# A hybrid encoder layer on one core: first keys' transpose later, own value buffers for every other of the last units, layer results stored by ScalarE, last row block in two column halves

## The chip, the cores and the metric

The kernel runs on one core of a Trainium2 chip. The engines of the core are TensorE (PE, with PEld for its weight loads), VectorE (DVE), ScalarE (ACT), GpSimd (POOL) and SyncE (SP), which in this kernel issues nearly all of the transfers; 16 DMA engines carry these out. Each engine works through its own list of instructions in order and waits on semaphores for the others. The metric is the device time of one launch in microseconds (us); less is better.

## The reference

Two sequences of 2048 tokens (prompt and sample, width 1024) go through one layer with the same weights:

```python
h = rms_norm(x, norm_w)
q_a, k_a, v_a, g_a, q_b, k_b, v_b, g_b = split(h @ w_in)      # 512 128 128 512 512 512 512 512
q_a, k_a = (partial_rope(rms_norm(u)) for u in (q_a, k_a))
o_a = windowed_gqa_sink(q_a, k_a, v_a, sink_a) * silu(g_a)    # 8 q heads, 2 kv heads, +-128 tokens
o_b = neighbourhood_attn(rms_norm(q_b), rms_norm(k_b), v_b, rpb_b) * silu(g_b)   # 8 heads, 64-wide grid, 8 rows x 16 columns
x = x + concat([o_a, o_b]) @ w_out
y = x + (p @ w_ple) * sigmoid(x @ w_ple_gate)                 # p: 256 wide
```

Everything is float32.

## The kernel before

All matrix products run as pairs of rounded numbers: each operand is split into a high and a low part (`[:, a]`, `[:, b]` with 0 and 1), and three of the four partial products are summed in PSUM. So "hi/lo" splits on ACT and DVE belong to every operand, and a product over 128 of the inner dimension takes three matmuls, shown as `x3`.

The program has three stages. **Stage A** (units f = 0 to 31, until about 708 us) takes one tile of 128 tokens per unit through group A: projections in `proj_a`, attention in `unit_a`. **Stage B** (units 32 to 95, until about 1821 us) does the same for group B, half of its 8 heads at a time, in `proj_b` and `unit_b`. **Stage C** (until the end) is the output projection and then the gate, in 8 groups of 7 products (Strassen's way of multiplying 2 x 2 blocks) with four row blocks `mi` each. A row block of 128 x 512 takes 12 matmuls on PE.

PE runs in the order in which the program is written. While PE works on the attention of a unit, it is handed matmuls of other work between the attention's steps: the projections of later units, as a stream that two tables of fractions of a unit (PLAN_A, PLAN_B) cut into pieces. From unit 90 on no projections are left, and the stream is `ple_ahead`: `p @ w_ple`, 8 row blocks for each of 8 tiles of 512 tokens. A row block is 6 matmuls into the PSUM tile `pple`, a copy by ACT into a buffer `ev` (L1003) and a store of 256 KB into the DRAM tensor `ple_d`, from which stage C reads it back at the end. Buffers `ev` come from two rings of 3 and 2; after stage B (`tail`) from another ring.

In the order of the other engines, `P(...)` marks instructions that keep their place in program order, and the rest is arranged by the tile scheduler by priorities and readiness.

The places that the change touches:

- `proj_a` and `keys_a`: the keys of unit f are normalised and rotated on POOL and DVE into `kt` (L517 to L520), and when `ka` matmuls of the same projection have passed, PE transposes them into `pkt` (L255) and ACT and DVE write them to `ks_a`. `ka` is 33 (KA), and 22 in the units in `last`.
- `unit_b`, `load_values` (L861 to L868): up to four loads of values, each 240 to 256 KB, from `v_d` into tiles `vw`, which lie in two rings, `vp` with 3 and `vr_` with 2 buffers. SP issues them. A unit's work on PE ends in `pob` matmuls, one group for each pair of heads, which need `vw` and the transposed probabilities `p_t`: PE transposes into `ptb`, ACT casts the high part (L894), DVE subtracts for the low part (L895).
- `prep_b` (L836 to L839): the queries of the next unit, from the PSUM tile `pqtb`: two times ACT (`q1b`), DVE (`q`) and POOL.
- `store_ple` (L976 to L982): the store of a copy `ev` goes out when the next one has been made, on SP.
- `product`, `result` and `behind_tanh` (L1213 to L1288): in stage C's gate groups the last sum of a row block is followed by ACT's tanh (L1273), and two DVE operations (L1283, L1284), which make the sigmoid, the product with `p @ w_ple` and the sum with x, out of it; then SP stores 256 KB of y (L1288). DVE's part of a row block is written behind the next row block's tanh, the last one's by a call at the end (L1325).

Of the kernel before, what the change touches and what calls it, by code (L numbers as in the profile page):

```python
# [11 lines left out]
F32 = mybir.dt.float32  # L12
F32R = mybir.dt.float32r
# [6 lines left out]
NT = SEQ // 128  # L20
# [80 lines left out]
def emit(ctx, tc, io):  # L101
# [382 lines left out]
    def proj_a(f):  # L484
        s, t = divmod(f, NT)
        xr, ms, (ssq, ee) = xt.pop(f), ms_a[:, f:f + 1], stats.pop(f)
        ka = 22 if f in last else KA
        early = 1 < f < 2 * NT - 1
        pk = ptile([128, 256], "pj" if f > 1 else "sc", "pk")
        for i, c in enumerate(project(pk, xr, lambda k, b: wx[:, k, b, :], 112)):  # L490
# [353 lines left out]
    def unit_b(f):  # L844
        half, st = divmod(f - 2 * NT, 2 * NT)
        s, j = divmod(st, NT)
        b, cb = divmod(j, 4)
        _, gs = held[f]
        r0, nr, c0, ncol, rows = window(b, cb)
        kc, nch = rows * ncol, nr // rows  # L850
        n = nr * ncol
        if cb != 2:
            off, _ = BIAS_OFF[(row_type(b), col_type(cb))]
            if not bt:
                bt.append(big([128, 2, 4, 512], F32, "bias"))
            bt.append(bt[0][:, len(bt) % 2])
            nc.sync.dma_start(bt[-1][:, :, :n], io["bias"][half][:, off:off + 4 * n].rearrange("p (h n) -> p h n", h=4))
        bias = bt[-1]
        vw = []

        def load_values():  # L861

            for j in range(nch):
                v = ap.tile([128, 4, 2 * HD], F32R, tag=("vp", "vr_")[j % 2], name="vw", bufs=3 - j % 2)
                nc.sync.dma_start(v[:kc].bitcast(F32).rearrange("p h d -> p (h d)"),
                                  v_d[half, s, cb][r0 + rows * j:r0 + rows * j + rows]
                                  .rearrange("r c h a d -> (r c) (h a d)"))
                vw.append(v)  # L868

        sees = [query_rows(b, cb, j) for j in range(nch)]  # L870
        order = sorted(range(nch), key=lambda j: sees[j][1] - sees[j][0])
        at = [16 * sum(z - a for a, z in sees[:j]) for j in range(nch + 1)]
        sm, p_ts, got = sm_tiles(), [], {}

        def sc(h):
            ps = ptile([128, 512], "sc", "scb")
            for j, q in enumerate(qs[f]):
                mm(ps[:, :n].rearrange("p (r c) -> p r c", c=ncol), q[h % 2][:, 128 * (h // 2):128 * (h // 2) + 128],
                   ks_b[h % 2][:, r0:r0 + nr, h // 2, c0:c0 + ncol], j == 0, j == 1)
            softmax(h, ps, n, bias[:, h, :n], sm)  # L880
            if h == 3:
                got["ex"] = exps(sm, hr_b[:, st:st + 1], gs)
                next(got["ex"])

        def pt(x):
            h = (0, 2, 1, 3)[x]
            pt = ptile([128, 512], "pt", "ptb")
            for j in order:

                c = at[j] - 16 * sees[j][0]  # L890
                tr(pt[:kc, c:c + 128], sm["s"][h][:, kc * j:kc * j + kc], rowwise)
            p_t = main.tile([128, 2, 512], F32R, tag="p_t", name="p_t", bufs=3)
            hi, lo, pf = p_t[:kc, 0, :at[-1]], p_t[:kc, 1, :at[-1]], pt[:kc, :at[-1]]
            nc.scalar.copy(hi, pf)  # L894
            nc.vector.tensor_tensor(out=lo, in0=pf, in1=hi.bitcast(F32), op=ALU.subtract)  # L895
            p_ts.append(p_t)

        def po(x):
            h = (0, 2, 1, 3)[x]
            e, i = h % 2, h // 2  # L900
            if i == 0:
                got["po"] = ptile([128, 2, 256], "ms", "pob")
            if x == 0:
                got["ot"] = ap.tile([128, 2, 2, 128], F32, tag="ot", name="otb", bufs=2)
            po, ot = got["po"], got["ot"]
            for j in order[::-1]:
                a, z = sees[j]
                mm(po[:, i, :].rearrange("p (a q) -> p a q", a=2)[:, :, 16 * a:16 * z], vw[j][:kc, h, :],
                   p_ts[x][:kc, :, at[j]:at[j + 1]], j == order[-1], j == order[0])
            if i == 1:  # L910
                a, z = 64 * e, 64 - 64 * e
                pq = po.rearrange("p i (a q) -> p i a q", a=2)
                nc.scalar.copy(ot[a:a + 64], pq[z:z + 64])  # L913
                nc.vector.tensor_tensor(out=ot[a:a + 64], in0=pq[a:a + 64], in1=ot[a:a + 64], op=ALU.add)  # L914

        def fin(_):
            pgt = ptile([128, 2, 128], "sc", "pgtb")
            for i in range(2):
                tr(pgt[:, i, :], sm["g2"][:, 128 * i:128 * i + 128], rowwise)
            o_t = ap.tile([128, 2, 128], F32, tag="o_t", name="o_tb", bufs=2)  # L920
            nc.gpsimd.tensor_tensor(out=o_t, in0=got["ot"][:, :, 0], in1=got["ot"][:, :, 1], op=ALU.add)
            nc.vector.tensor_tensor(out=o_t, in0=pgt, in1=o_t, op=ALU.mult)
            nc.sync.dma_start(ob_d[s][b, :, 2 * half:2 * half + 2, cb, :], o_t)
        return {"sc": sc, "pt": pt, "po": po, "fin": fin, "prep": lambda _: nxt(f),
                "exp": lambda _: (next(got["ex"]), load_values())}


# [45 lines left out]
            early[name].append(w)  # L973
        del coming[:n]

    made = []  # L976

    def store_ple(n):

        for dst, ev in made[:n]:  # L980
            nc.sync.dma_start(dst, ev)
        del made[:n]  # L982

    def ple_ahead(n, tail=False):

        load_p(n + 1)
        for m in range(KT):
            if m % 4 == 3 and (n < 3 or m == 3):
                load_coming()
            ps = ptile([128, TW], "pj", "pple")  # L990
            if m == 5 and n + 1 < len(tiles):
                split_p(n + 1)
            flush("p0")
            for k in range(2):
                w, c = early["p"][2 * (m // 4) + k], 128 * (m % 4)
                for i, (a, b) in enumerate(((0, 0), (0, 1), (1, 0))):
                    mm(ps, w[:, a, c:c + 128], p_rs[n][:, k, b], k == 0 and i == 0, k == 1 and i == 2)
                    yield 215
            if tail:
                ev = main.tile([128, TW], F32, tag="s", name="ev", bufs=SB)  # L1000
            else:
                ev = ap.tile([128, TW], F32, tag=("ev", "sq")[m // 2 % 2], name="ev", bufs=3 - m // 2 % 2)
            P(nc.scalar.copy(ev, ps))  # L1003
            store_ple(1)
            if tail:
                nc.sync.dma_start(ple_d[n][:, m], ev)
            else:
                made.append((ple_d[n][:, m], ev))

    qs = {}  # L1010

# [105 lines left out]
    with tc.tile_pool(name="c", bufs=1, reuse_waits="tile") as op:  # L1117
# [92 lines left out]

        acc = {}

        def product(m, mi):  # L1213

            n, i = divmod(m, 7)
            w = ws[groups[n][0]][STEPS[i]]
            key = ("c" if i in (1, 4, 5) else "a", mi)
            if i in (0, 1, 4):
                tag = ("ms" if mi < 2 else "pj") if i == 0 else "sc" if i == 1 or mi < 3 else "pj"
                acc[key] = ptile([128, TW], tag, "acc" + key[0])  # L1220
            ps, c = acc[key], 128 * mi
            for k in range(4):
                o = opds[m, k]
                for j, (a, b) in enumerate(((0, 0), (1, 0), (0, 1))):
                    pinned(nc.tensor.matmul(ps, w[k][:, a, c:c + 128], o[:, b], start=i in (0, 1, 4) and k == 0 and j == 0,  # L1225
                                            stop=k == 3 and j == 2, skip_group_check=True))
            return ps

# [50 lines left out]
        def behind_tanh():  # L1279

            if ends:
# [5 lines left out]
                s, u = divmod(n, 4)  # L1287
                P(nc.sync.dma_start(io["y_t"][s].rearrange("(m p) t -> p m t", p=128)[:, m, TW * u:TW * u + TW], r))  # L1288

        load_raw(0, 0)  # L1290
        drain(ple_ahead(AHEAD, True))
        load_raw(0, 1)
# [15 lines left out]
        for m in range(7 * len(groups)):  # L1308
            n, i = divmod(m, 7)
            if i >= 3:  # L1310
                load_raw(n + 1, i - 3)
            if n == 0:
                flush({2: "0s2", 3: "0s1", 4: "0s3", 6: "0s4"}.get(i))
            for mi in range(4):
                if (n == 0 and i in (1, 2, 3, 5)) or (n == n_o - 1 and i >= 3) or (n == n_o and i < 3):
                    pump()
                combos(n, i, mi)
                for k in range(2 * mi, 2 * mi + 2) if mi < 2 else ():
                    piece(m + 1, k)
                result(n, i, mi, product(m, mi))  # L1320
            if n == n_o - 1:
                load_q(1, STEPS[i])
            elif n == n_o and i < 3:
                flush("1" + STEPS[i + 4])
        behind_tanh()  # L1325


def _band():
# [73 lines left out]
```

## Time and profile before

| | us |
|---|---|
| median of 3 runs | 2472.81 (2471.73 to 2474.23) |
| the profiled execution | 2471.11 |
| its span in the profile | 2469.3 |
| PE busy | 2453.1 |
| DVE busy | 1703.8 |
| ACT busy | 1413.5 |
| POOL busy | 856.4 |

A profile row of the timeline has a start and a duration in us, the engine, the line, the operation, what it writes and reads, the tile's shape and a count of merged instructions. A bracket tells how long the engine had been idle before it and what it then waited for. PE, DVE, ACT, POOL are engines, SPq and ACTq are the issuing of transfers by SP and ACT. The granted clock of PE is 1.00 in all of the stages but the tail. Matmuls overlap at their ends, so a group of n takes n times its step and not n times the duration of one.

### The profile page before, as it was taken

How to read it: one execution, taken by the hardware profiler on the slowest of the kernel's cores; microseconds unless marked ns; L12 is line 12 of the kernel's file. 1: busy time of each engine (PE TensorE's matmuls, PEld its weight loads, DVE VectorE, ACT ScalarE, POOL GpSimd, SP SyncE). 2: the span in 40 equal slices, each digit the busy share in tenths (PEclk: the TensorE clock that was granted, in tenths of full speed). 3: DMA queues.
4: the chain of work that ended last, by engine and by line, in shares of the span. 5: the costliest groups of instructions: out<-in, count | busy, mean ns of one | idle time of the engine just before them, and what ended most of it. 6: DMA issues, size and time to landing. Idle time of an engine off the chain costs nothing.

```text
span 2469.3 us, 40516 instructions
## 1 busy us (share of the span) xinstructions
PE 2453.1 (99%) x13050; PEld 2074.2 (84%) x13050; DVE 1703.8 (69%) x4212; ACT 1413.5 (57%) x3407; POOL 856.4 (35%) x1363
## 2 busy tenths in 40 slices
PE   9999999999999999999999999999999999999999
PEld 8888888888888888888888888888888888888887
DVE  7777777777765666666666666666537655677776
ACT  7777776777664665656655566665763212344433
POOL 4555555555543544454544444443110000000000
PEclk9999999999999999999999999999999999999999
DMA  6332223232255565556955566567977445756765
GB/s 227 122 103 93 95 88 103 95 101 88 95 180 164 169 191 183 183 163 196 313 183 179 173 218 202 193 202 230 311 251 269 156 166 175 270 180 207 251 222 170
DMA packets 243172, 442.01 MB, mean 179 GB/s; under 512 B 27888, under 2 KB 82320, under 8 KB 237712
## 3 DMA queue, kind: packets, MB, share of 16 engines
q1 hardware_dynamic: 242672, 439.42, 54.4%
q8 instruction: 104, 1.70, 0.3%
q14 instruction: 108, 0.88, 0.1%
q10 hardware_dynamic: 288, 0.01, 0.0%
HBM read 309.29 MB, written 134.23 MB: 180 GB/s over the span
## 4 chain that ended last, share of the span: by engine, by line
PE 93%; DVE 2%; DMA 2%; ACT 2%; POOL 1%; issue 0%; SPq 0%; DVEq 0%; ACTq 0%; POOLq 0%
PE acca L1225 14%; PE pvg L252 14%; PE pqk L252 14%; PE accc L1225 10%; PE pg L252 7%; PE pq L252 6%; PE scb L252 4%; PE ptb L255 3%; PE pob L252 3%; PE pk L252 3%; PE po L252 3%; PE pple L252 3%; PE sc L252 3%; PE pt L255 2%; DMA vw<-v_d 1%; PE pktb L255 1%
## 5 line engine op out<-in xcount | busy, mean ns | idle before, releaser
L284 ACT ACTIVATE s<-s,nm 128x320 f32<-128x320 f32 (+6 forms) x512 | 294.4, 576 | 317.8 <-DVE nm L279 198.5
L252 PE MATMUL pvg<-wb,xr 128*128 128x512 f32 x1536 | 461.8, 407 | 0.0
L252 PE MATMUL pqk<-wa,xr 128*128 128x512 f32 x1536 | 443.0, 411 | 0.0
L252 PEld LDWEIGHTS pqk<-wa,xr 128*128 128x128 f32 x1536 | 266.0, 189 | 37.0
L252 PEld LDWEIGHTS pvg<-wb,xr 128*128 128x128 f32 x1536 | 266.7, 189 | 31.2 <-DMA wb<-sp_1wb 0.4
L1207 ACT CAST opd<-raw 128x512 fp32r<-128x512 f32 x224 | 131.5, 619 | 271.2 <-PE acca L1225 118.6
L353 POOL TENSOR_TENSOR xr<-stx,xr 128x512 fp32r<-128x512 f32 x186 | 238.9, 1294 | 100.8 <-ACT xr L352 76.0
L1208 DVE TENSOR_TENSOR opd<-raw,opd 128x512 fp32r<-128x512 f32 x224 | 146.4, 685 | 146.6 <-ACT opd L1207 146.6
L252 PE MATMUL pg<-wb,xr 128*128 128x512 f32 x768 | 233.2, 409 | 1.0 <-DVE vv L510 1.0
L252 PE MATMUL pq<-wa,xr 128*128 128x512 f32 x768 | 219.3, 400 | 0.0
L268 DVE CUSTOM_DVE_ANT_0 s<-scb,bias 128x288 f32<-128x288 f32 (+3 forms) x256 | 142.0, 555 | 104.8 <-PE scb L252 101.5
L137 POOL TENSOR_TENSOR yb<-vrb,power 128x8 f32<-128x8 f32 x64 | 106.4, 1662 | 222.7 <-DVE vrb L783 197.1
L1225 PE MATMUL accc<-opd,wb 128*128 128x512 f32 x768 | 176.7, 389 | 0.0
L1225 PE MATMUL acca<-opd,wa 128*128 128x512 f32 x768 | 175.5, 389 | 0.0
L1225 PE MATMUL acca<-opd,s 128*128 128x512 f32 x768 | 175.4, 389 | 0.0
L1225 PEld LDWEIGHTS acca<-opd,wa 128*128 128x128 f32 x768 | 144.2, 188 | 29.9
L1225 PEld LDWEIGHTS accc<-opd,wb 128*128 128x128 f32 x768 | 144.2, 188 | 29.9
L1225 PEld LDWEIGHTS acca<-opd,s 128*128 128x128 f32 x768 | 144.2, 188 | 29.9
L914 DVE TENSOR_TENSOR otb<-pob,otb 64x512 f32<-64x512 f32 x128 | 88.1, 689 | 114.0 <-ACT otb L913 112.4
L252 PEld LDWEIGHTS pob<-p_t,vw 128*128 128x128 f32 (+2 forms) x832 | 132.5, 189 | 27.6 <-DVE p_t L895 4.6
L252 PEld LDWEIGHTS pq<-wa,xr 128*128 128x128 f32 x768 | 135.1, 189 | 17.3
L711 DVE TENSOR_TENSOR pr<-pt,pr 128x512 fp32r<-128x512 f32 (+2 forms) x248 | 135.6, 549 | 17.3 <-ACT pr L709 14.1
(168 smaller groups left out, 5166.8 us busy)
## 6 DMA issues: line engine op xcount, KB each, us to landing
stx<-x_b SPq DMA_DIRECT2D x128, 256.0 KB
vw<-v_d SPq DMA_DIRECT2D x112, 256.0 KB
stx<-x_a SPq DMA_DIRECT2D x64, 256.0 KB
stn<-x_n SPq DMA_DIRECT2D x64, 256.0 KB
v_d<-vb SPq DMA_DIRECT2D x64, 256.0 KB
ple_d<-ev SPq DMA_DIRECT2D x64, 256.0 KB
xres<-x_r SPq DMA_DIRECT2D x64, 256.0 KB
x_d<-r SPq DMA_DIRECT2D x64, 256.0 KB
```

Source lines behind the costliest of these rows:

```text
L137: nc.gpsimd.tensor_tensor(out=y, in0=v, in1=power.broadcast_to([128, n]), op=ALU.pow)
L252: pinned(nc.tensor.matmul(out, lhsT, rhs, start=start, stop=stop))
L255: pinned(nc.tensor.transpose(out, in_, eye))
L268: nc.vector.tensor_tensor_reduce(out=s, in0=ps[:, :n], in1=bias, scale=1.0, scalar=-3.0e38, op0=ALU.add, op1=ALU.max, accum_out=sm["mx"][: ...
L284: ex = nc.scalar.activation(ss[i], ss[i], AF.Exp, bias=nm[:, i:i + 1], accum_out=den[:, i:i + 1])
L353: low.tensor_tensor(out=lo, in0=raw, in1=hi.bitcast(F32), op=ALU.subtract)
L711: nc.vector.tensor_tensor(out=pr[r, 1, to], in0=pt[r, c], in1=pr[r, 0, to].bitcast(F32), op=ALU.subtract)
L914: nc.vector.tensor_tensor(out=ot[a:a + 64], in0=pq[a:a + 64], in1=ot[a:a + 64], op=ALU.add)
L1207: P(nc.scalar.copy(hi, v))
L1208: P(nc.vector.tensor_tensor(out=lo, in0=v, in1=hi.bitcast(F32), op=ALU.subtract))
L1225: pinned(nc.tensor.matmul(ps, w[k][:, a, c:c + 128], o[:, b], start=i in (0, 1, 4) and k == 0 and j == 0, stop=k == 3 and j == 2, skip_gro ...
```

## The change

Four edits. First, the keys of unit 0 are transposed 11 matmuls later (`ka` 44 in place of 33). Second, in units 90, 92 and 94 the four value tiles lie in a tile of their own (`vw4`, a free ring of one buffer). Third, the 64 stores of `p @ w_ple` are issued by ACT, right behind the copy in program order, in place of SP one copy later; `store_ple` goes. Fourth, the very last row block is computed in two halves of 256 columns, each with its own tanh, two DVE operations and a store of 128 KB; DVE's part of the row block before stands between the first half's matmuls and its tanh.

```diff
-        ka = 22 if f in last else KA
+        ka = 22 if f in last else 44 if f == 0 else KA
...
+            spare = f >= 6 * NT - 6 and f % 2 == 0
+            if spare:
+                four = ap.tile([128, 4, 4, 2 * HD], F32R, tag="raw", name="vw4", bufs=1)
             for j in range(nch):
-                v = ap.tile([128, 4, 2 * HD], F32R, tag=("vp", "vr_")[j % 2], name="vw", bufs=3 - j % 2)
+                v = four[:, j] if spare else \
+                    ap.tile([128, 4, 2 * HD], F32R, tag=("vp", "vr_")[j % 2], name="vw", bufs=3 - j % 2)
...
-    made = []
-
-    def store_ple(n):
-
-        for dst, ev in made[:n]:
-            nc.sync.dma_start(dst, ev)
-        del made[:n]
...
             P(nc.scalar.copy(ev, ps))
-            store_ple(1)
-            if tail:
-                nc.sync.dma_start(ple_d[n][:, m], ev)
-            else:
-                made.append((ple_d[n][:, m], ev))
+            P(nc.scalar.dma_start(ple_d[n][:, m], ev))
...
-        def product(m, mi):
+        def product(m, mi, cols=slice(0, TW)):
...
-                    pinned(nc.tensor.matmul(ps, w[k][:, a, c:c + 128], o[:, b], start=i in (0, 1, 4) and k == 0 and j == 0,
+                    pinned(nc.tensor.matmul(ps[:, cols], w[k][:, a, c:c + 128], o[:, b, cols],
+                                            start=i in (0, 1, 4) and k == 0 and j == 0,
                                             stop=k == 3 and j == 2, skip_group_check=True))
...
+        def last_result(n, m):
+
+            _, g = groups[n]
+            s, u = divmod(2 * g + 1, 4)
+            r = op.tile([128, TW], F32, tag="r", name="r", bufs=9 - SB)
+            x, y = loaded[2:4]
+            V = nc.vector
+            for i in range(2):
+                c = slice(TW // 2 * i, TW // 2 * i + TW // 2)
+                ps = product(m, 3, c)
+                if i == 0:
+                    behind_tanh()
+                P(nc.scalar.activation(r[:, c], ps[:, c], AF.Tanh, scale=0.5))
+                P(V.scalar_tensor_tensor(out=r[:, c], in0=r[:, c], scalar=1.0, in1=x[:, c], op0=ALU.add, op1=ALU.mult))
+                P(V.scalar_tensor_tensor(out=r[:, c], in0=r[:, c], scalar=0.5, in1=y[:, c], op0=ALU.mult, op1=ALU.add))
+                P(nc.sync.dma_start(io["y_t"][s][384:512, TW * u + c.start:TW * u + c.stop], r[:, c]))
...
-                result(n, i, mi, product(m, mi))
+                if (m, mi) == (7 * len(groups) - 1, 3):
+                    last_result(n, m)
+                else:
+                    result(n, i, mi, product(m, mi))
...
-        behind_tanh()
```

How instructions move is shown at three places. First PE in unit 0, around the transpose of the keys (`pkt`), which stands among the gate projection's matmuls `pg`; before:

```order
L252 MATMUL pg<-wb_115,xr 128x512 x3
L252 MATMUL pg<-wb_116,xr 128x512
L255 MATMUL pkt<-ident,kt 128x128
L252 MATMUL pg<-wb_116,xr 128x512 x2
L252 MATMUL pg<-wb_117,xr 128x512 x3
L252 MATMUL pg<-wb_118,xr 128x512 x3
```

And now:

```order
L252 MATMUL pg<-wb_115,xr 128x512 x3
L252 MATMUL pg<-wb_116,xr 128x512 x3
L252 MATMUL pg<-wb_117,xr 128x512 x3
L252 MATMUL pg<-wb_118,xr 128x512 x3
L252 MATMUL pg<-wb_119,xr 128x512 x3
L255 MATMUL pkt<-ident,kt 128x128
L252 MATMUL pg<-wb_120,xr 128x512 x3
```

The transpose has moved from behind the first matmul with `wb_116` to behind the last with `wb_119`, 11 matmuls later. Second ACT in unit 91, from the unit's last exponentials (L284) on; before:

```order
L284 ACTIVATE s,den<-s,nm 128x360 x2
L1003 COPY ev<-pple 128x512
L836 ACTIVATE q1b<-pqtb,wk 64x256
L894 CAST p_t<-ptb 120x288
L836 ACTIVATE q1b<-pqtb,wk 64x256
L1003 COPY ev<-pple 128x512
L894 CAST p_t<-ptb 120x288
```

And now (L999 is the copy that was L1003, L1000 the store, L898 the cast that was L894):

```order
L284 ACTIVATE s,den<-s,nm 128x360 x2
L999 COPY ev<-pple 128x512
L836 ACTIVATE q1b<-pqtb,wk 64x256
L1000 DMA ple_d_323<-ev 128x512
L836 ACTIVATE q1b<-pqtb,wk 64x256
L999 COPY ev<-pple 128x512
L898 CAST p_t<-ptb 120x288
L1000 DMA ple_d_323<-ev 128x512
L898 CAST p_t<-ptb 120x288
```

Both `q1b` and a second copy now stand ahead of the first cast of `p_t`, and two stores stand among them. Third PE at its end, the last row block; before:

```order
L1225 MATMUL acca<-opd,wa_25801 128x512 x3
L1225 MATMUL acca<-opd,wa_25803 128x512 x3
L1225 MATMUL acca<-opd,wa_25805 128x512 x3
L1225 MATMUL acca<-opd,wa_25807 128x512 x3
```

And now, with the waits shown (Activation_49 is a semaphore that ACT raises):

```order
L1217 MATMUL acca<-opd,wa_25798 128x256 x3
L1217 MATMUL acca<-opd,wa_25800 128x256 x3
L1217 MATMUL acca<-opd,wa_25794 128x256 [waits Activation_49]
L1217 MATMUL acca<-opd,wa_25794 128x256 x2
L1217 MATMUL acca<-opd,wa_25796 128x256 x3
L1217 MATMUL acca<-opd,wa_25798 128x256 x3
L1217 MATMUL acca<-opd,wa_25800 128x256 x3
```

Four groups of three of half the width stand twice, and the second half's first matmul waits for ACT. Value loads stay on SP, ahead of whose list no stores of `ple_d` stand any more.

## The prediction

> **What bounds the kernel now.** I read the busy times of the page first, then the busy time of each engine by stretch, then the waits of PE, and last the rows of the three places that the change touches.
>
> ```profile
> span 2469.3 us, 40516 instructions
> PE 2453.1 (99%) x13050; PEld 2074.2 (84%) x13050; DVE 1703.8 (69%) x4212; ACT 1413.5 (57%) x3407; POOL 856.4 (35%) x1363
> ```
>
> PE is busy for 2453.1 of 2469.3 us, so all idle time of the bound engine together is 16.2 us, 0.66% of the span. The change takes no matmul work away. It can only gain what lies in those 16.2 us, and it can lose as much as it makes PE wait. Where the idle time lies is told by the stretches (columns: window, its length, then busy time of PE, PEld, DVE, ACT, POOL, granted clock, DMA share, GB/s):
>
> ```profile
> 0.00:45.00 45.00, 41.80 (x209) 34.65 (x210) 33.05 (x88) 31.66 (x69) 20.20 (x40) 1.00 0.73 253
> 45.00:1738.00 1693.00, 1688.11 (x9563) 1440.96 (x9562) 1192.98 (x3315) 1093.41 (x2790) 821.67 (x1294) 1.00 0.50 160
> 1738.00:1768.00 30.00, 28.64 (x157) 23.32 (x156) 15.35 (x40) 20.07 (x46) 4.86 (x10) 1.00 1.01 352
> 1768.00:1821.00 53.00, 51.96 (x294) 43.73 (x293) 30.56 (x81) 39.36 (x95) 8.98 (x18) 1.00 0.68 232
> 1821.00:2440.00 619.00, 618.82 (x2732) 512.23 (x2731) 408.89 (x655) 219.59 (x393) 0.74 (x1) 1.00 0.62 209
> 2440.00:2469.30 29.30, 23.78 (x105) 19.35 (x104) 22.98 (x36) 9.40 (x16) 0.00 (x0) 0.96 0.76 251
> ```
>
> PE idles 3.20 us in the first 45, 4.89 in the next 1693, 1.36 and 1.04 in units 90 to 95, 0.18 in nearly all of stage C and 5.52 in the tail. The change touches the first, the third with the fourth, and the last. PE's waits put names to them (total, times, longest):
>
> ```profile
> PE pob L252 <- DMA vw<-v_d: 1.8, 5, 0.6
> PE pkt L255 <- POOL kt L520: 1.2, 1, 1.2
> PE pob L252 <- DVE p_t L895: 0.9, 2, 0.6
> ```
>
> **Part one, the keys' transpose.** One transpose goes 11 matmuls later on PE, and nothing is added.
>
> ```profile
> 23.91 2.43 PE L252 MATMUL pg<-wb,xr 128*128 128x512 f32 x10
> 25.98 2.73 DVE L152 SCALAR_TENSOR_TENSOR wb<-ws,nw,wb 128x512 fp32r<-128x512 f32 x4
> 27.24 0.26 POOL L520 TENSOR_TENSOR kt<-r 128x32 f32<-128x32 f32 x1
> 27.55 0.33 PE L255 MATMUL pkt<-ident,kt 128*128 128x128 f32 x1 [1.22 <-POOL kt L520]
> ```
>
> POOL writes `kt` until 27.50. The matmuls ahead of the transpose end at 26.34 and PE stands for 1.22 us. In the changed order 11 more stand ahead of it, so PE reaches it after about 21, at 23.91 + 21 x 0.24 = 28.95 (0.243 each in the first row), when `kt` has been there for 1.4 us. What could be late next are the weights `wb` of those matmuls, which DVE splits until 25.98 + 2.73 = 28.71, four in a row at 0.68 each: the k-th of the four is there by 25.98 + 0.68k, and PE needs a new one only every 3 matmuls (0.73 us), so they arrive about as they are used. The term is **-1.2 us**, with bounds of -1.3 (wait plus its semaphore) and 0 (the wait goes over to `wb`).
>
> **Part two, values and stores in units 90 to 95.** Own buffers let three of the six units load their values without waiting for an older tile, and 64 stores of 256 KB leave SP, behind which the value loads now stand. That takes the cause of the 1.8 us away. But the stores are put on ACT in program order, and the order of ACT and DVE around the softmax changes with it: the second `q1b` now stands ahead of the first cast of `p_t`, and it has to wait for DVE's first `q`, which reads the same buffer. In unit 91 before:
>
> ```profile
> 1760.89 0.56 ACT L1003 COPY ev<-pple 128x512 f32<-128x512 f32 x1
> 1761.36 0.47 ACT L836 ACTIVATE q1b<-pqtb,wk 64x256 fp32r<-64x256 f32 x1
> 1761.72 0.38 ACT L894 CAST p_t<-ptb 120x288 fp32r<-120x288 f32 x1
> 1761.86 0.47 DVE L837 SCALAR_TENSOR_TENSOR q<-pqtb,wk,q1b 64x256 fp32r<-64x256 f32 x1
> 1762.26 0.44 DVE L895 TENSOR_TENSOR p_t<-ptb,p_t 120x288 fp32r<-120x288 f32 x1
> 1762.37 0.47 ACT L836 ACTIVATE q1b<-pqtb,wk 64x256 fp32r<-64x256 f32 x1 [0.26 <-DVE q L837]
> 1764.17 0.35 PE L252 MATMUL pob<-p_t,vw 120*128 120x256 f32 x1 [0.64 <-DMA vw<-v_d]
> 1765.06 0.43 PE L252 MATMUL pple<-p_r,wa 128*128 128x512 f32 x1
> ```
>
> Count from E, the start of the copy behind the unit's exponentials (1760.89). Before, both halves of the first `p_t` are there at 1762.70 = E + 1.8. In the new order: copy 0.47, `q1b` 0.47 (to E + 0.95), DVE's `q` to E + 1.45, second `q1b` to E + 1.95, then the cast of `p_t` to about E + 2.35 and DVE's part of it, behind the second `q`, to **E + 2.9**. In units 91, 92 and 94 the next copy stands ahead of the cast as well, 0.45 more: **E + 3.35**. PE then needs 0.04 for the semaphore and 0.3 to 0.4 for the 3 or 4 `pob` matmuls until its next `pple`. In units 90, 92, 93 and 94 the rows before are:
>
> ```profile
> 1746.37 0.56 ACT L1003 COPY ev<-pple 128x512 f32<-128x512 f32 x1
> 1750.00 0.67 PE L252 MATMUL pple<-p_r,wa 128*128 128x512 f32 x2
> 1775.19 0.57 ACT L1003 COPY ev<-pple 128x512 f32<-128x512 f32 x1
> 1778.71 0.67 PE L252 MATMUL pple<-p_r,wa 128*128 128x512 f32 x2
> 1790.10 0.56 ACT L1003 COPY ev<-pple 128x512 f32<-128x512 f32 x1
> 1792.38 0.45 PE L252 MATMUL pple<-p_r,wa 128*128 128x512 f32 x1
> 1803.21 0.57 ACT L1003 COPY ev<-pple 128x512 f32<-128x512 f32 x1
> 1805.75 0.45 PE L252 MATMUL pple<-p_r,wa 128*128 128x512 f32 x1
> ```
>
> New time of that `pple` less the old: unit 90, 1746.37 + 3.1 (its store's issue stands ahead of the exponentials) + 0.45 = 1749.92, -0.1; unit 91, 1760.89 + 3.35 + 0.35 = 1764.59, -0.5; unit 92, 1775.19 + 3.35 + 0.34 = 1778.88, +0.2; unit 93, 1790.10 + 2.87 + 0.34 = 1793.31, +0.9; unit 94, 1803.21 + 3.35 + 0.34 = 1806.90, +1.15; unit 95 about 0. So where values were late the gain is mostly taken back, and where they were in time (93, 94) `p_t` is late next. The term is **+1.7 us**. Its lower bound is all idle time of both stretches, -2.4. Queued behind the cast on ACT are the next casts and copies, for which PE waits only through `pob` again.
>
> The issues themselves: ACT takes 0.41 us in the one row that shows it issuing a transfer.
>
> ```profile
> 0.72 0.41 ACTq L117 DMA_DIRECT2D nw<-norm_w  x1
> ACT q1b L836 <- DVE q L837: 37.2, 44, 2.0
> ACT ev L1003 <- DMA ple_d<-ev: 7.3, 2, 6.3
> ```
>
> Most of the 64 stand where ACT waits anyway: between the two `q1b` it has some 0.5 us to wait for DVE, and after 1821 ACT is busy for a third of the time (219.59 of 619). Four stand between the exponentials or casts that PE waits for; if they are not covered they cost 4 x 0.41 = 1.6. I take 0 for them, and +1.7 + 1.6 = +3.3 as the upper bound of the part. The 64 issues that leave SP shorten nothing that PE waits for except the value loads.
>
> **Part three, the last row block in halves.** The last product and what follows it:
>
> ```profile
> 2452.74 11.04 PE L1225 MATMUL acca<-opd,wa 128*128 128x512 f32 x48
> 37.00 3.04 PE L252 MATMUL pk<-wx,xr 128*128 128x256 f32 x24
> 2463.82 0.60 ACT L1273 ACTIVATE r<-acca 128x512 f32<-128x512 f32 x1 [2.12 <-PE acca L1225]
> 2465.18 0.69 DVE L1284 SCALAR_TENSOR_TENSOR r<-r,xres 128x512 f32<-128x512 f32 x1
> 2463.36 2.87 SPq L1288 DMA_DIRECT2D y_t<-r  x2
> 1745.84 0.42 DVE L922 TENSOR_TENSOR o_tb<-pgtb,o_tb 128x256 f32<-128x256 f32 x1 [0.90 <-POOL o_tb L921]
> ```
>
> A matmul of 512 columns takes 0.23, of 256 columns 3.04/24 = 0.127. The last product starts at 2463.78 - 12 x 0.23 = 2461.0; its first half ends at 2462.55. Both halves lie in one PSUM tile, and in the changed order the first matmul of the second half waits for ACT: it waits for the whole tile's reader, the tanh (an ACT operation of half the width, some 0.4). So PE starts again at 2463.0 and ends at 2464.5, 0.7 later than now; then tanh to 2464.95 and two DVE operations of 0.42 to 2465.8, against 2465.87 now. The chain gains about nothing up to the store. The store itself is 128 KB instead of 256: from DVE's end to the span's end it is 3.43 us now, and 128 KB at the window's 251 GB/s over a share of 0.76 (330 GB/s) are 0.40. Term **-0.4 us**; bounds -2.2 (the halves do not wait, -0.5, and the store takes half, -1.7) and +0.4 (an issue of the first half's store in the way). [...]
>
> **Sum.** -1.2 + 1.7 - 0.4 = +0.1 on the profiled execution's 2471.1 (1.8 us more than its span), so 2471.2. The median of the runs, 2472.8, stands 1.7 above that execution: I forecast **2472.9 us**, no change that can be told.
>
> **Rivals.** First, faster: ACT and DVE have the first `p_t` in time after all (the casts may start as soon as PE's transposes are in, and q1b's wait be short), and the values' gain stays: -1.2 - 2.4 - 0.4 = -4.0, 2468.8 us. For it speaks that DVE is busy for only 15.35 of 30 us there; against it that `q1b` waited for `q` 44 times, as the row above has it. Second, slower: a copy that now stands directly ahead of the first cast (91, 92, 94) finds its buffer `ev` still being stored, and PE waits for the store. The longest such wait now is 6.3 us, and the DMA engines are busy for all of 1738 to 1768 (1.01); from the store landing some 3 us after its issue on, it decides. Then 0.1 + 6.3 more: 2479.2 us. Against it speaks that both waits of the row lie after 1840, and that a store goes out one copy earlier than before. Third, the four issues are not covered: +1.6, 2474.5 us; for it speaks that ACT is the engine that `p_t` waits for. Fourth, the loads land no sooner, since the engines that move them are full: units 90 to 92 wait as before, 93 and 94 for `p_t`: -1.6 + 2.1 = +0.5, 2473.3 us. [...] The share of 1.01 agrees with it; the own buffers are what speaks against.
>
> **How the numbers follow.** Forecast 0.52, first rival 0.16, second 0.08, third 0.17, fourth 0.07. A measurement of this kernel can tell about 0.2%, 4.9 us: faster means below 2467.9, slower above 2477.8. The first rival lies 0.9 above the lower line and passes it in half of its cases (0.08), the forecast with everything at its lower bounds in a few (0.02): 0.10. The second rival is slower (0.08), and so are the upper ends of the third and of the forecast (0.06): 0.14. The rest is 0.76. The range reaches from the first rival's middle less 1.3 to the upper line: 2467.5 to 2478.0.
>
> **What would show it.** In the changed profile: the `pkt` wait gone from PE's list; PE's `pob` waits for `vw` gone and in their place about 1 us each for `p_t` by DVE in units 93 and 94; a gap of some 0.45 us of PE between the last two halves, and a store that ends some 3 us after the last DVE operation. The forecast is wrong if `p_t` is ready by E + 1.8 again, if ACT shows waits for `ple_d` before 1821, or if the idle time of PE between 45 and 1738, where nothing is changed by hand, moves by more than a us.

## The result and the profile after

The changed kernel takes 2484.27 us (median of 4 runs, 2482.57 to 2486.75) against 2472.66 us before (4 runs): a ratio of 1.005 with a 95% interval of 1.0038 to 1.0062. It is slower, by 11.6 us, and outside the predicted range of 2467.5 to 2478.0.

The busy times by stretch of the changed kernel, as they were shown of the kernel before (window, length, busy PE, PEld, DVE, ACT, POOL, granted clock, DMA share, GB/s):

```profile
0.00:45.00 45.00, 43.33 (x208) 36.12 (x209) 33.42 (x87) 31.27 (x68) 20.16 (x40) 1.00 0.73 250
45.00:1738.00 1693.00, 1688.86 (x9567) 1441.47 (x9566) 1191.57 (x3315) 1093.89 (x2793) 821.98 (x1295) 1.00 0.51 161
1738.00:1768.00 30.00, 26.61 (x141) 21.92 (x140) 14.86 (x38) 18.51 (x43) 4.86 (x10) 0.94 1.01 340
1768.00:1821.00 53.00, 50.17 (x278) 41.85 (x277) 28.85 (x77) 37.24 (x88) 8.03 (x16) 1.00 0.58 196
1821.00:2440.00 619.00, 612.55 (x2700) 505.20 (x2699) 407.15 (x655) 220.82 (x396) 2.15 (x3) 1.00 0.62 209
```

The start gains: PE idles 1.67 us there in place of 3.20. The loss lies in two places, in units 90 to 95 (3.39 and 2.83 us idle in place of 1.36 and 1.04) and behind 1821, where PE hardly idled before (6.45 in place of 0.18). In the first of them the granted clock is 0.94, too. The list of PE's waits has two new heads, in which the waits for `vw` and for `kt` no longer stand:

```profile
PE pob L252 <- DVE p_t L899: 7.0, 7, 2.6
PE pple L252 <- ACT ev L999: 5.6, 4, 3.2
```

Where they lie is seen in PE's timeline (the bracket: idle time and what ended it):

```profile
1750.64 0.67 PE L252 MATMUL pob<-p_t,vw 128*128 128x256 f32 x4 [2.62 <-DVE p_t L899]
1767.04 0.57 PE L252 MATMUL pob<-p_t,vw 120*128 120x256 f32 x3 [0.76 <-DVE p_t L899]
1780.94 0.56 PE L252 MATMUL pob<-p_t,vw 96*128 96x256 f32 x3 [0.63 <-DVE p_t L899]
1795.73 0.56 PE L252 MATMUL pob<-p_t,vw 128*128 128x256 f32 x3 [1.17 <-DVE p_t L899]
1810.38 0.55 PE L252 MATMUL pob<-p_t,vw 128*128 128x256 f32 x3 [1.02 <-DVE p_t L899]
1842.80 11.17 PE L252 MATMUL pple<-p_r,wa 128*128 128x512 f32 x48 [1.20 <-ACT ev L999]
1863.13 4.38 PE L252 MATMUL pple<-p_r,wa 128*128 128x512 f32 x12 [3.18 <-ACT ev L999]
```

Units 91 to 94 wait 0.6 to 1.2 us each, as forecast. Unit 90 waits 2.62 us, and behind the last unit PE waits for copies, which was not forecast. What ACT does in unit 90, with DVE's first `q` between, and in unit 91 (ACTq is ACT issuing a transfer):

```profile
1747.01 0.47 ACT L836 ACTIVATE q1b<-pqtb,wk 64x256 fp32r<-64x256 f32 x1
1747.51 0.48 DVE L837 SCALAR_TENSOR_TENSOR q<-pqtb,wk,q1b 64x256 fp32r<-64x256 f32 x1 [0.67 <-ACT q1b L836]
1748.65 0.33 ACTq L1000 DMA_DIRECT2D ple_d<-ev  x1
1749.02 0.47 ACT L836 ACTIVATE q1b<-pqtb,wk 64x256 fp32r<-64x256 f32 x1 [1.55 <-DMA wb<-sp_oa]
1749.52 0.47 ACT L898 CAST p_t<-ptb 128x368 fp32r<-128x368 f32 x1
...
1763.64 0.56 ACT L999 COPY ev<-pple 128x512 f32<-128x512 f32 x1
1765.12 0.47 ACT L836 ACTIVATE q1b<-pqtb,wk 64x256 fp32r<-64x256 f32 x1 [0.54 <-DVE q L837]
1766.09 0.41 ACT L898 CAST p_t<-ptb 120x288 fp32r<-120x288 f32 x1
```

In unit 90 ACT stands still for 1.2 us until 1748.65, and what ends it is a load of weights (`wb`). A `q1b` doesn't need weights: it is the store ahead of it that waits. The order of the changed program, with the waits, shows for what (DMAHW5 is there the semaphore of a load of `wb`); ACT around that place:

```
L836 ACTIVATE q1b<-pqtb,wk 64x256 [waits PE_49]
L1000 DMA ple_d_322<-ev 128x512 [waits DMAHW5_49,Activation_49]
L836 ACTIVATE q1b<-pqtb,wk 64x256 [waits DVE_49]
L898 CAST p_t<-ptb 128x368 [waits PE_49]
```

In the changed program the transfers of SP and ACT report their end on eight semaphores, DMAHW0 to DMAHW7, in turn, and 53 of ACT's 64 stores wait for the semaphore on which they report themselves, so for an earlier transfer on it (the first expectation below counts 52). In the program before, all 64 stores wait in the same way on SP, ahead of SP's next transfers; on ACT the casts and copies stand behind them, here for the 1.2 us. Unit 91 has no such wait: there the second `q1b` waits 0.54 us for DVE and the cast starts late, as forecast (both halves of `p_t` at 1766.99 = E + 3.35).

So the 2.62 us of unit 90 have two parts. DVE's first `q` ends at 1747.99, and the second `q1b` could have started some 0.04 us behind it, as in unit 91; it starts at 1749.02. About 1.0 us is the store's wait for the load. The other 1.6 us or so would have been there without it: they come from the order, in which the cast stands behind both `q1b`.

One more cost comes with the two long waits, shown by PE's clock in windows of 2 us behind the wait of unit 90:

```profile
1750.00:1752.00 2.00, 1.36 (x8) 1.13 (x9) 1.10 (x3) 0.84 (x2) 0.00 (x0) 0.95 1.05 250
1752.00:1754.00 2.00, 2.00 (x8) 1.78 (x7) 0.53 (x1) 1.00 (x3) 0.00 (x0) 0.50 1.08 351
1754.00:1756.00 2.00, 2.00 (x10) 1.74 (x8) 1.18 (x4) 1.94 (x4) 0.00 (x0) 0.69 1.07 401
1756.00:1758.00 2.00, 2.00 (x11) 1.78 (x10) 1.78 (x4) 1.17 (x2) 0.00 (x0) 1.00 1.03 393
```

The granted clock falls to one half some 1.2 us after PE has started again and stays there for about 3.4 us (in windows of 0.5 us: 1751.8 to 1755.2). PE counts as busy, but three matmuls of 512 columns that take 0.78 us in the kernel before (1751.10 to 1751.88) take 1.42 there (1752.65 to 1754.07). Half of the 3.4 us, an estimate from the clock of 0.50, is 1.7 us lost on top of the 2.62. Behind the wait of 3.18 us the same is seen at 1864.5 to 1867.9.

### The profile page after: what moved, and what is told of

Same layout as the page of the kernel before. It is cut to its first block, busy times and chain, and to the rows that moved or that the text cites. A ratio compares the mean times of both kernels' runs of the same rounds, so it can differ in the third digit from the quotient of the medians.

```text
span 2482.7 us, 40499 instructions
## 1 busy us (share of the span) xinstructions
PE 2459.4 (99%) x13062; PEld 2078.1 (84%) x13062; DVE 1703.4 (69%) x4214; ACT 1414.7 (57%) x3408; POOL 857.2 (35%) x1363
## 4 chain that ended last, share of the span: by engine, by line
PE 90%; DVE 3%; ACT 2%; DMA 2%; issue 1%; POOL 1%; SPq 0%; ACTq 0%; DVEq 0%
PE acca L1217 14%; PE pvg L252 14%; PE pqk L252 14%; PE accc L1217 10%; PE pq L252 6%; PE pg L252 6%; PE scb L252 4%; PE pk L252 3%; PE ptb L255 3%; PE pob L252 3%; PE po L252 3%; PE sc L252 3%; PE pt L255 2%; PE pple L252 2%; ACT s L284 1%
## 5 line engine op out<-in xcount | busy, mean ns | idle before, releaser
L284 ACT ACTIVATE s<-s,nm 128x320 f32<-128x320 f32 (+6 forms) x512 | 294.4, 576 | 317.0 <-DVE nm L279 197.6
L1217 PE MATMUL acca<-opd,wa 128*128 128x512 f32 (+1 forms) x780 | 176.2, 386 | 0.5 <-ACT r L1295 0.5
```

Of the source, the lines that this page charges most:

```text
L284: ex = nc.scalar.activation(ss[i], ss[i], AF.Exp, bias=nm[:, i:i + 1], accum_out=den[:, i:i + 1])
L1217: pinned(nc.tensor.matmul(ps[:, cols], w[k][:, a, c:c + 128], o[:, b, cols], start=i in (0, 1, 4) and k == 0 and j == 0, stop=k == 3 and j ...
```

## Experiments

The milestones by which the runs are compared are three times of each profiled execution, in us: the start of the long run of `pple` matmuls behind the last unit, the start of stage C's first product, and the span.

| kernel | units end | stage C starts | between | span |
|---|---|---|---|---|
| before | 1821.08 | 1853.83 | 32.75 | 2469.3 |
| changed | 1826.37 | 1867.31 | 40.94 | 2482.7 |
| stores_sp | 1817.49 | 1850.47 | 32.98 | 2466.1 |
| act_units | 1826.56 | 1861.15 | 34.59 | 2476.5 |
| act_lagged | 1820.11 | 1861.88 | 41.77 | 2477.2 |
| probe | 1823.34 | 1857.28 | 33.94 | 2474.4 |
| pool_own | 1817.41 | 1854.22 | 36.81 | 2469.8 |

Against stores_sp, which has the other three edits, ACT's stores cost 8.9 us in the units and 8.0 behind them.

**Only the stores on ACT (stores_act).** The kernel before with the third edit alone.

> The kernel before with the third edit alone: the 64 stores are issued by ACT behind each copy. Theory A: a store waits at its issuer until an earlier transfer that holds the same one of eight completion semaphores has landed (the order of the changed program shows such a wait, DMAHW, at 52 of the 64), and on ACT the copies and casts stand behind it. Then this part alone carries the whole loss: 13 us of it plus the 1.0 us that the moved transpose gained, 2484 to 2488 us. Theory B: ACT loses the 0.33 us of each issue and the changed order of q1b and p_t; it gives the same time here and is told apart by the run with an ACT operation in place of the issue. Theory C: the loss comes from the other edits (value tiles, halves): then 2471 to 2474 us.

Measured: 2488.75 us (2486.87 to 2489.92), ratio 1.0062 (1.0047 to 1.0077) against 2473.24. The third edit alone carries more than the whole loss, 15.5 us, a little over the upper end of theory A. Theory C falls.

**All but the stores on ACT (stores_sp).**

```diff
-            P(nc.scalar.dma_start(ple_d[n][:, m], ev))
+            store_ple(1)
+            if tail:
+                nc.sync.dma_start(ple_d[n][:, m], ev)
+            else:
+                made.append((ple_d[n][:, m], ev))
```

> The changed kernel with the stores back on SP, one copy later, as before; the other three edits stay. Theories A and B: the loss goes, and the transpose (-1.0 us as the changed trace shows by 708 us) and the value tiles (-0.5 to -1.8) are left: 2470 to 2471.5 us. Theory C: 2480 us or more.

Measured: 2469.51 us (2467.92 to 2471.71, 11 runs), ratio 0.9985 (0.9976 to 0.9993): 3.7 us faster than before, slightly better than expected. Of the kernels here only own_values and busy_own below come out the same. In units 90 to 95 PE is busy nearly throughout (same columns as above):

```profile
1738.00:1768.00 30.00, 30.00 (x172) 25.50 (x171) 17.22 (x44) 22.08 (x50) 4.88 (x10) 1.00 1.03 350
1768.00:1821.00 53.00, 52.37 (x293) 44.23 (x293) 31.16 (x81) 39.29 (x94) 9.73 (x19) 1.00 0.65 223
```

**ACT's time without a transfer (act_busy, busy_own).** Behind each copy ACT makes an idle one; first in the kernel before, then in stores_sp.

```diff
             P(nc.scalar.copy(ev, ps))
+            P(nc.scalar.copy(ev[:, :192], ev[:, :192]))
             store_ple(1)
```

> The kernel before, stores on SP; behind each copy ACT copies 192 columns of the buffer onto themselves (estimated 0.3 us, about the 0.33 us of an issue, and with the same wait for its own copy), no wait for a transfer. Theory A: ACT's time matters little, 2472 to 2475 us. Theory B: most of the loss is here too, 2480 us or more.

> The run stores_sp with ACT's 192-column copy behind each copy, no transfer on ACT. Theory A: ACT's time as such is covered, 2469.5 to 2472 us. Theory B (ACT's time for 64 issues is the loss): 2476 us or more.

Measured: act_busy 2475.64 us (2473.36 to 2479.11), ratio 1.0011 (1.0001 to 1.0020), 2.4 us over before, just above theory A's range; busy_own 2469.48 us (2468.66 to 2470.24), the same as stores_sp. The extra copies take some 0.33 us each (in act_busy ACT is busy for 1434.56 us in place of 1413.5, over 64 of them). So ACT's time as such is covered, and with it falls that half of theory B. The other half, the changed order, is not tested here: in both programs the first cast of `p_t` stands ahead of the second `q1b`, as before the change. What act_busy loses shows in its waits of PE between 1738 and 1880 (in an execution of 2479.11 us, 3.5 above its median, so the rows show more than the usual loss):

```profile
PE pob L252 <- DMA vw<-v_d: 3.7, 3, 3.0
PE pple L252 <- ACT ev L1003: 0.8, 1, 0.8
```

The values are late, as in the kernel before; with own value tiles the extra ACT work costs nothing.

**POOL as the issuer (stores_pool, pool_own).** The first is the kernel before, the second the changed kernel, both with this line:

```diff
-            P(nc.scalar.dma_start(ple_d[n][:, m], ev))
+            P(nc.gpsimd.dma_start(ple_d[n][:, m], ev))
```

> The kernel before with the 64 stores issued by POOL behind each copy, in program order. These stores use semaphores of their own and the order shows far fewer waits for transfers. Theory A: nothing that PE waits for stands behind them, 2471 to 2475 us. If instead the stores' own bytes, going out one copy earlier and beside SP's queue, delay the loads, the time is 2480 us or more here too.

> The changed kernel with its stores issued by POOL in place of ACT (own value tiles and halves kept). POOL's stores use eight semaphores of their own; none of them waits for a load. Theory A (ACT stands at a semaphore shared with SP's transfers): the loss goes, 2469 to 2472 us. Theory E (the stores going out a copy earlier, beside SP's queue, delay the value loads, as in the run with POOL and without own tiles): 2476 us or more.

Measured: stores_pool 2482.24 us (2479.84 to 2483.93), ratio 1.0037 (1.0023 to 1.0050), against theory A's forecast. PE's timeline of that run has the reason:

```profile
1754.01 0.40 PE L252 MATMUL pob<-p_t,vw 128*128 128x256 f32 x1 [3.98 <-DMA vw<-v_d]
1756.32 0.69 PE L252 MATMUL pob<-p_t,vw 128*128 128x128 f32 x2 [1.12 <-DMA vw<-v_d]
```

Values again, and worse than before. SP's issues there and in the kernel before, first stores_pool:

```profile
1738.16 4.70 SPq L972 DMA_DIRECT2D wb<-sp_oa  x5
1743.81 2.51 SPq L865 DMA_DIRECT2D vw<-v_d  x4
```

and before:

```profile
1737.27 0.38 SPq L972 DMA_DIRECT2D wb<-sp_oa  x1
1739.40 1.59 SPq L972 DMA_DIRECT2D wb<-sp_oa  x2
1742.43 1.30 SPq L865 DMA_DIRECT2D vw<-v_d  x3
```

With the stores gone from SP, five loads of weights stand in a row ahead of the values in place of three (two of the stores lie between those), and the first value load goes out 1.4 us later. That SP's order and not the stores' bytes made the values late is a reading of these rows; the run itself came out as expected of the bytes. With own tiles, in pool_own, the order and the buffers both differ. pool_own measures 2472.68 us (2471.64 to 2474.76), ratio 0.9999 (0.9989 to 1.0009), 0.7 above theory A's range. Its units end at 1817.41, as early as with SP: the stores' bytes, another issuer and the earlier issue cost nothing in the units, so theory E falls for them. Theory A is not shown by it alone. In both programs 56 of POOL's 64 stores wait as well, on POOL and only for POOL's earlier stores (so the waits are not fewer, as the first expectation has it), and ACT's order has the first cast of `p_t` ahead of the second `q1b` again: the run lacks both the stores' waits on ACT and the late cast. The 3.8 us more than stores_sp lie behind the units, where copies wait for their buffers' stores; ACT's waits in that run between 1738 and 1880:

```profile
ACT ev L999 <- DMA ple_d<-ev: 13.8, 10, 2.5
```

**The wait without the bytes (probe).** stores_sp with a transfer of 512 bytes on ACT behind each copy, into a scratch tensor.

```diff
             P(nc.scalar.copy(ev, ps))
+            P(nc.scalar.dma_start(probe[n][m:m + 1], ev[0:1, :128]))
             store_ple(1)
```

> The run stores_sp with, behind each copy, a transfer of 512 bytes (one row of 128 numbers into a scratch tensor) issued by ACT; the 256 KB stores stay on SP. The order of ACT has the first cast of p_t ahead of the second q1b, as before, and 58 of the 64 small transfers wait for one of the eight shared semaphores. Theory A: the wait costs, not the bytes and not the order: 2478 us or more. Theory D (the forecast's: the cast of p_t moved behind both q1b): 2469.5 to 2472 us. Theory E: 2469.5 to 2472 us.

Measured: 2476.76 us (2475.07 to 2479.54, 10 runs), ratio 1.0017 (1.0008 to 1.0026), 7.3 above stores_sp. Theories D and E, which gave 2469.5 to 2472, fall as sole causes; theory A's 2478 is missed by 1.2 us. The loss lies in the units (5.9 of it, some 3 of them, an estimate, from 6.8 us of PE at a granted clock of 0.50 around a wait), with a new kind of row in ACT's waits:

```profile
ACT p_t L898 <- DMA vw<-v_d: 3.6, 1, 3.6
ACT ev L1008 <- DMA vw<-v_d: 1.4, 1, 1.4
```

No cast or copy on ACT reads `vw`. These are the small transfers, waiting for value loads of SP on a shared semaphore, with ACT's casts behind them. Behind the units the probe costs only 1.0 us, so it doesn't reproduce that part.

**Stores on ACT only in the units (act_units).**

```diff
+            if tail:
+                nc.sync.dma_start(ple_d[n][:, m], ev)
+            else:
+                P(nc.scalar.dma_start(ple_d[n][:, m], ev))
```

> The changed kernel with ACT's stores only in units 90 to 95 (40 of the 64); the 24 behind the last unit are SP's again. The changed trace loses 5.9 us up to the end of the last unit and 8.2 us behind it. Theory A: about 6 us above stores_sp, 2475 to 2477 us, and no wait of PE for a copy behind the last unit longer than 1 us. If the part behind the units is only the first part's backlog, 2470 to 2472 or 2483 us.

Measured: 2476.23 us (2474.85 to 2478.28), ratio 1.0014 (1.0004 to 1.0023). The time is as expected; one wait of 1.52 us for a copy is left behind the units where none over 1 us was expected. So the two halves of the loss are separate: 6.7 us come with the 40 stores in the units, and 8.0 more (2484.27 less 2476.23; 6.2 between the two profiled executions) with the 24 behind them.

**ACT's stores, casts first (act_lagged).** In the units each store stands behind the next copy, which puts the first cast ahead of the second `q1b`. 46 of the 64 stores still wait for an earlier transfer.

```diff
         for dst, ev in made[:n]:
-            nc.sync.dma_start(dst, ev)
+            P(nc.scalar.dma_start(dst, ev))
...
             if tail:
-                nc.sync.dma_start(ple_d[n][:, m], ev)
+                P(nc.scalar.dma_start(ple_d[n][:, m], ev))
```

> The changed kernel with ACT still the issuer, but in units 90 to 95 each store stands behind the next copy (as SP's did before). The order of ACT then has the first cast of p_t ahead of the second q1b again; the waits for shared semaphores stay, and the stores behind the last unit are as in the change. The changed trace has 3.6 us of PE's waits for p_t in units 91 to 94, put down to the order, and 2.6 in unit 90 with a half clock behind it, put down to the semaphore. Theory A with D for its part: the 3.6 us go and the rest stays, 2479 to 2482 us. If the order alone were the loss in the units: 2475 to 2477 us (the part behind the units, 8 us, above stores_sp's 2469.5 less nothing).

Measured: 2480.15 us (2477.25 to 2482.77), ratio 1.0031 (1.0020 to 1.0042), inside theory A's range with D for its part. PE's timeline:

```profile
1752.40 0.67 PE L252 MATMUL pob<-p_t,vw 128*128 128x256 f32 x4 [1.73 <-DVE p_t L899]
...
1820.11 28.33 PE L252 MATMUL pple<-p_r,wa 128*128 128x512 f32 x120
1850.13 1.66 PE L252 MATMUL pple<-p_r,wa 128*128 128x512 f32 x6 [1.69 <-ACT ev L1007]
1857.29 4.74 PE L252 MATMUL pple<-p_r,wa 128*128 128x512 f32 x12 [2.31 <-ACT ev L1007]
1861.88 11.05 PE L1229 MATMUL acca<-opd,wa 128*128 128x512 f32 x48
```

Units 91 to 94 no longer wait for `p_t` at all. Unit 90 waits 0.29 us for the first cast, and 1.73 us later on, behind a store that holds ACT up for 2.87 us until a load of values has landed. Unlike the 2.62, the 1.73 have no half clock behind them; the waits behind the units stay. By the milestones the units lose 2.6 us to stores_sp in place of 8.9, so 6.3 us of the loss in the units go with the order, the half clock among them.

**The other edits one by one (own_values, no_own_values).** The kernel before with the own value tiles alone, and the changed kernel with stores on SP and without these tiles (the later transpose and the halves).

> The kernel before with the second edit alone (own value tiles in units 90, 92 and 94, stores on SP). PE's waits for vw (1.8 us of the idle 2.4 us in units 90 to 95) go: 2470.5 to 2471.5 us, about 2.4 under before by the milestones of stores_sp. If the value tiles only move the wait to p_t: 2472 to 2473.5 us.

> The changed kernel without own value tiles and with the stores on SP: the later transpose and the halves alone. Terms of the prediction: -1.2 and -0.4 (seen in the changed trace: -1.0 by 702 us and -0.4 from the last product on): 2471 to 2472.2 us.

Measured: own_values 2469.19 us (2467.50 to 2472.25, 11 runs), ratio 0.9987 (0.9978 to 0.9996) against 2472.47; better than expected by a us. no_own_values 2471.23 us (2469.21 to 2473.18, 11 runs), ratio 0.9995 (0.9986 to 1.0004): 1.2 us under before as expected, but not told from no change by its interval.

## Why the prediction was wrong

**What held.** The bound by PE and its idle time held. The wait of 1.2 us for the transposed keys is gone, and by 702 us the changed trace is 1.0 us ahead. The value tiles take the wait for `vw` away, worth what the first rival gave them (2.4 us, all idle time there; 3.3 measured alone). The late cast behind both `q1b` is as the prediction counted it: `p_t` at E + 3.35 in unit 91, and waits of 0.76, 0.63, 1.17 and 1.02, together 3.6 us, in units 91 to 94, which went in act_lagged, with the cast back ahead of the second `q1b`. With the gain of the values in it, that term was +1.7. The last row block does what was worked out, with its gap of 0.47 us for the tanh:

```profile
2476.26 0.38 ACT L1295 ACTIVATE r<-acca 128x256 f32<-128x256 f32 x1 [0.83 <-PE acca L1217]
2476.70 1.69 PE L1217 MATMUL acca<-opd,wa 128*128 128x256 f32 x12 [0.47 <-ACT r L1295]
2479.30 0.42 DVE L1297 SCALAR_TENSOR_TENSOR r<-r,xres 128x256 f32<-128x256 f32 x1
```

From the end of the last DVE operation, 2479.72, to the end of the span are 2.98 us in place of 3.43, so the store gains 0.45. The chain up to it is 0.12 longer, and from the start of the last product's four row blocks to the end of the span 16.23 us in place of 16.56 are left: the term of -0.4 was -0.3.

**What failed** is one step of part two: "Most of the 64 stand where ACT waits anyway [...] I take 0 for them". The step priced an issue by its duration, 0.41 us (0.33 measured), and asked only whether ACT had that much time. It didn't ask what the issuing instruction itself waits for. The prediction's second rival had a copy that waits on ACT for its buffer's store, in units 91, 92 and 94; such waits came, but behind the units (five, 8.9 us of ACT's time). The wait of the store itself for another transfer was in none of the cases, though the program's order, with waits, already showed it. None of the prediction's three signs of being wrong came either: `p_t` was not ready by E + 1.8, ACT's list of waits has none for `ple_d` before 1821, and PE's idle time between 45 and 1738 moved from 4.89 to 4.14 us.

What the runs put in place of the 0, with stores_sp as the base: in the units, 3.6 us of the order in units 91 to 94, 1.6 of the order and 1.0 of a store's semaphore in unit 90, and an estimated 1.7 for the clock behind that wait make 7.9 of the 8.9 us. The prediction had counted the order (its +1.7 against the -2.4 of the values' gain is 4.1), so in the units it missed some 4.8 us. Behind the units, where its reason was that ACT is busy for only a third of the time, it had nothing: PE's waits for copies sum to 5.6 us there, with 1.7 for the clock 7.3 of 8.0. The prediction took the clock as 1.00 throughout, which is 3.4 us of its error by the same estimate (two times 1.7).

That a store's wait on ACT costs time in the units is shown by the probe, which has neither the bytes nor the late cast. That the larger part of the change's own loss there goes with the order is shown by act_lagged, though its stores also come to wait for other transfers. The split of unit 90's wait is read from the rows of one execution. Behind the units the division is only read, too. ACT there, ahead of the two waits of PE that end at 1858.29 and 1863.13:

```profile
1857.29 0.33 ACTq L1000 DMA_DIRECT2D ple_d<-ev  x1
1857.65 0.58 ACT L999 COPY ev<-pple 128x512 f32<-128x512 f32 x1 [2.10 <-PE pple L252]
1860.05 0.33 ACTq L1000 DMA_DIRECT2D ple_d<-ev  x1
1860.42 2.18 ACT L1199 CAST opd<-raw 128x512 fp32r<-128x512 f32 x4 [2.18 <-DMA s<-sums]
1862.50 0.58 ACT L999 COPY ev<-pple 128x512 f32<-128x512 f32 x1
```

The casts don't read `s`; the store ahead of them waits for that load, and by the program's order the store at 1857.29 waits for an earlier store (the copy behind it reads a row block that PE had finished by 1853.97). So of the 5.6 us some 3.2 are stores that wait on ACT (0.99 and 2.2 of the 3.18), 1.0 the four casts that then stand ahead of the copy, and 1.5 copies that wait for their buffers' stores. No run separates these three: POOL's stores cost 3.8 us there without the shared semaphores, and the probe 1.0.

The fourth rival, in which the loads land no sooner because the engines that move them are full, did not come. They are as full as before from 1738 to 1768 (a share of 1.01 in both kernels), and no wait for `vw` stands in the list of the changed kernel. The own tiles and not the other issuer brought the values in time: with them the units end at 1817.41 us with POOL as the issuer (pool_own) and at 1817.49 with SP.

## What to carry to other kernels

What a store cost here on ACT was not the 0.33 us of its issue but what it waited for (1.2 us of ACT's time in unit 90) and what its place in the order delayed (3.6 us of PE's waits in units 91 to 94): before moving transfers from an engine that only issues to one that computes, read the semaphores that they wait for in the order of the new program, and count what stands behind them. Where a bundle of edits is slower, run it without the suspected edit first: here three of four edits gained 3.7 us and the fourth lost some 15. In these runs the single waits of PE of 2.31 to 4.05 us had 3.4 or 6.8 us at a granted clock of 0.50 behind them, by the estimate above another 1.7 or 3.4 us, which belongs in their price.

## What the runs showed of the hardware

The half clock behind a wait was not expected. Single waits of PE and what followed at a granted clock of 0.50, from the timelines and from windows of 0.5 us (for act_units from longer ones: 0.94 on average from 1738 to 1768, as in the changed kernel, and 1.00 from 1826 to 1870):

| run | wait, us | half clock behind it, us |
|---|---|---|
| act_units | 1.52 (behind the units) | none |
| act_lagged | 1.73 (unit 90) | none |
| probe | 1.73, with 0.67 some 3 us ahead of it | 6.8, the first 0.7 of it still in the wait |
| act_lagged | 2.31, with 1.53 and 1.69 ahead | 3.4 |
| changed | 2.62 | 3.4 |
| act_units | 2.62 | some 3.4 |
| act_busy | 3.03 | 3.4 |
| changed | 3.18 | 3.4 |
| stores_act | 3.47 | 3.4 |
| stores_pool | 3.98, with 1.12 behind it | 6.8 |
| stores_act | 4.05 | 3.4 |

In these rows the half clock lasts for 3.4 or 6.8 us, and not longer behind the longer waits: 3.4 behind 2.31 and behind 4.05. Of the two waits of 1.73 us one has it behind it and the other has not. What decides whether the clock falls, and when, is not shown by these runs.
